# Landing times of 18 kinds of load and store in a planner that orders the five queues of a hybrid encoder layer

## The chip, the core and the metric

The kernel runs as one program on one core of a Trainium2 chip. The time is device microseconds (us) of one execution, and the figure used for the kernel before is the median of three executions. A core has five engines that work on their own instruction queues: TensorE (PE, matrix products; PEld is its loading of the stationary operand), VectorE (DVE), ScalarE (ACT), GpSimd (POOL) and SyncE (SP). Here SP issues all transfers between the main memory and the core's own memory. Each queue is worked off in the order in which it was written; an instruction that waits holds up everything behind it in its queue.

## The reference, cut to what matters

One layer, one sequence of 2048 positions, 1024 features, everything in float32. The input is normalised, projected once, and split between two groups of heads; their outputs are projected back and added to the input.

```python
h = rms_norm(x, norm_w[l])
proj = h @ w_in[l]
(dn_q, dn_k, dn_v, dn_z, dn_beta, dn_decay, sw_q, sw_k, sw_v, sw_z) = split(proj, cuts)
dn = gated_deltanet_bidir(dn_q, dn_k, dn_v, dn_beta, dn_decay, ...)   # 4 heads of 128
dn = rms_norm(dn, dn_out_norm_w[l]) * silu(dn_z)
sw = windowed_gqa_with_sinks(sw_q, sw_k, sw_v, ...) * silu(sw_z)      # 8 query heads of 64, window 128
x = x + concatenate([dn, sw]) @ w_out[l]
```

The delta-rule heads first pass q, k and v through a convolution of width 5. Then, chunk by chunk, a triangular matrix built from k, the decay and beta is inverted, and a state of 128x128 is carried along the sequence, once forward and once backward:

```python
t_inv = triangular_solve(eye + m, eye)
v_new = u_i - w_i @ state
o = (q_i * exp(g_i)) @ state + a_i @ v_new
state = state * exp(g_last) + k_dec.T @ v_new
```

## The kernel before, in words

The kernel is written as a program for the five queues, first without regard to what should come when; at the end a planner in the same file, `set_order`, lays down the order of every queue.

Phase A (`phase_a`) works in two halves of 1024 positions. Rows of x come in as tiles `xr` (for the sums of squares, and in the very first block also for transposition on PE), columns of x as tiles `xt`; both become the pairs `xhi`/`xlo`, from which every projection takes three products. Weights come in as `ws_...`. Windowed attention is interleaved with the convolution pairs (`pf_c`) and the gates (`pf_z`) as filling for PE. Results that phase B needs go to the main memory: `kq_d`, `v_d`, `zdn_d`, `zsw_d`, `mix_sw`.

Phase B (`phase_b`) handles the four delta-rule heads one after the other. For each head h:

- `pre_front(h)` runs over four groups of 512 positions. Each group loads `kq` (512 KB, two buffers), `vt` and two `dc` (decay matrices; for head 0 they were stored ready, for the others a row is loaded to all partitions), transposes k, q and v on PE (`tr` L674, `trv` L711), forms `gh` (L694), scales it on DVE into `ma` (L703), and stores half of `ma` to `m_d` (L708).
- `solve(h)` loads the diagonal blocks from `m_d` as `X` and `L` (L731, L732), solves 31 steps on DVE (L741, L745) and stores `x_d` (L746).
- `invert(h)` loads `xc` from `x_d` (L757), copies blocks on POOL and forms five products per group on PE (`pi`, L772).
- `scan(h)` walks 16 chunks in both directions. A step loads `kqc` (L810), forms `pk`, `py`, `po` on PE, and updates the state on DVE (L833). At the end `post` loads the gate `zt` (L880) and stores `mix_dn` (L882).

So a head is a chain through the main memory: `kq`, then `m_d`, `X`/`L`, `x_d`, `xc`, and then its scan. Heads alternate between two sets of `ma` buffers, so `pre_front(h+2)` follows scan(h). Between these, units of the output projection of the attention part fill PE: a unit loads `mxs`, sometimes `zcs`, and `xrs`, makes 12 products of 128x512 (`pcs`, L599 to L601) and stores `part`; its weights come in as `woss`. At the very end `out_dn` loads `mxd` and `xrd`, makes 12 products twice (`pcd`, L561 to L563) and stores the output; its weights come in as `wosd`.

The planner `set_order` collects all instructions, finds which depends on which, including those that must wait until a buffer is free, and gives each a duration (`cost`; 500 ns for an issue on SP). It then plays the program through forward and backward several times as a list scheduler: of the instructions that are ready on an engine, the one comes next whose time in the pass before demands it. The shortest plan of the last five forward passes is written into the queues as the order. What is planned is only the order: on the chip every instruction waits for its real inputs.

An instruction that depends on a transfer is ready, in the plan, when the issue has begun and the planned bus has become free, plus the 500 ns of the issue, plus a lag:

```python
LAG = {"PE": 205, "DVE": 140, "Activation": 160, "Pool": 120, "SP": 2400}
move[k] = count / piece * (8 + 0.148 * piece) / 16
lag = LAG[eng[k]] + move[k] + late[k] if k < n else 0
```

Here `count` is the number of elements and `piece` the number of them that lie side by side (at most 2048), so `move` is a time in ns from the size and the grain of the transfer, and `late` is 2000 for loads that spread one row over all partitions, else 0. The planned bus is busy for `move` with each transfer.

Of the kernel before, what the change touches and what calls it, by code (L numbers as in the profile page):

```python
# [927 lines left out]


ENGINES = ("PE", "DVE", "Activation", "Pool", "SP")  # L930
LAG = {"PE": 205, "DVE": 140, "Activation": 160, "Pool": 120, "SP": 2400}
SAME = {"PE": 0, "DVE": 115, "Activation": 130, "Pool": 120, None: 0}

# [4 lines left out]
def set_order(tc):  # L938


    insts, boundaries = [], []
    for i in tc.nc.cur_bb.bb.instructions:
        eng = str(i.engine).split(".")[1]
        if i.opcode == "TilePoolBoundary":
            boundaries.append(str(i))
        elif eng in ENGINES:
            insts.append((i, eng))
# [3 lines left out]
    def aps(l):  # L951
        return [a.bass_ap for a in l if hasattr(a, "bass_ap")]

    def size(a):
        r = 1
        for _, c in list(a.ap)[1:]:
            r *= c
        return r

    def run(a):  # L960
        inside = a.tensor.name in tiles and "DRAM" not in str(tiles[a.tensor.name].space)
        r = 1
        for step, c in reversed(list(a.ap)[1:] if inside else list(a.ap)):
            if step != r:
                break
            r *= c
        return min(r, 2048)
# [89 lines left out]
    for x in sorted((x for x in tc.tiles if x.tag in home and x.name in used), key=lambda x: used[x.name][0]):  # L1057
        name, bufs = home[x.tag]
        users.setdefault(name, []).extend(used[x.name])
        k = used[x.name][0]  # L1060
# [25 lines left out]
    for x in used:  # L1086
        k = used[x][0]
# [32 lines left out]
    move, late = [0.0] * total, [0.0] * total  # L1120
    nxt, prv = [[] for _ in range(total)], [[] for _ in range(total)]
    for k in range(total):
        if eng[k] == "SP":
            a = aps(insts[k][0].outs)[0]
            count = a.ap[0][1] * size(a)
            piece = min(run(x) for x in aps(insts[k][0].ins) + [a])
            move[k] = count / piece * (8 + 0.148 * piece) / 16
            spread = [x.ap[0][0] == 0 for x in aps(insts[k][0].ins)]
            late[k] = 2000 * any(spread)
        lag = LAG[eng[k]] + move[k] + late[k] if k < n else 0  # L1130
        if eng[k] == "PE" and not insts[k][0].is_transpose and "float32r" not in str(insts[k][0].ins[0].dtype):
            lag += 40
        if eng[k] == "Activation" and len(aps(insts[k][0].outs)) > 1:
            lag += 90
        for s in succ[k]:
            if eng[s] == eng[k] != "SP":
                nxt[k].append((s, SAME[eng[k]] * ((k, s) in wrote)))
            else:
                nxt[k].append((s, lag))
        for s in started[k] if k < n else ():  # L1140
            nxt[k].append((s, None))
        for s, d in nxt[k]:
            prv[s].append((k, d))
# [30 lines left out]
    def plan(order, forward):  # L1174
        to, back = (nxt, prv) if forward else (prv, nxt)
        left, at = [len(x) for x in back], [0.0] * total
        later, ready = {e: [] for e in ENGINES}, {e: [] for e in ENGINES}
        free, queue = dict.fromkeys(ENGINES, 0.0), {e: [] for e in ENGINES}
        begin, bus, held = [0.0] * total, 0.0, 0.0
# [24 lines left out]
        for _ in range(n):  # L1204
            t, e = min(
                (free[e] if ready[e] else max(free[e], later[e][0][0]), e) for e in ENGINES if ready[e] or later[e]
            )
# [38 lines left out]
    info = mybir.DependencyInfo(mybir.DependencyClass.NoSync, mybir.DependencyReason.DATA)  # L1246
    for e in ENGINES:
        for a, b in zip(queue[e], queue[e][1:]):
# [60 lines left out]
```

## Time and profile before

| | |
|---|---|
| median of 3 executions | 1278.94 us (1277.84 to 1281.57) |
| the profiled execution | 1274.25 us, span 1272.5 us from first to last instruction |
| mean granted TensorE clock | 0.992 |
| transfers | 205.34 MB, mean 161 GB/s over the span |
| busy DVE, ACT, POOL | 889.5, 703.2, 507.4 us |

Read the span in three parts: a start-up of some 20 us, phase A to about 660 to 770 us, and phase B after it. The timeline gives for each group of instructions its start, its time, its engine, the line of the kernel, the tile written and the tiles read; a bracket at the end gives the idle time of the engine just before, and what ended it. An "x4" behind a row means four instructions merged. PE products are pipelined: the next one starts before the time shown for the one before has run out, so the distance of starts is the better measure.

### The profile page before, as it was taken

The numbers are of one execution on the slowest core, as the hardware profiler recorded it, in microseconds if no ns is written. First come the engines' busy times: TensorE is split into PE (matmuls) and PEld (weight loads), VectorE is DVE, ScalarE is ACT, GpSimd is POOL, SyncE is SP. The second block draws the span as 40 slices with busy tenths as digits, with TensorE's granted clock in tenths as the row PEclk, the third lists the DMA queues.
The fourth block names the chain that finished last, engine by engine and source line by source line (L and its number), as shares of the span: only waits on it lengthen the run. The fifth ranks groups of instructions, "written<-read, shape, count | busy, mean of one in ns | idle before, by whom it ended". The sixth has DMA issues, their size and how long they took to land.

```text
span 1272.5 us, 22253 instructions
## 1 busy us (share of the span) xinstructions
PE 1219.4 (96%) x7066; PEld 1044.4 (82%) x7066; DVE 889.5 (70%) x2154; ACT 703.2 (55%) x2105; POOL 507.4 (40%) x893
## 2 busy tenths in 40 slices
PE   6999999999999999999999998998799899999998
PEld 6998877788889998787788787887688789798876
DVE  4422387999975589999986573788488879557333
ACT  6321254776644677776654425858557955566210
POOL 1330044666613398665221306613672651641000
PEclk9999999999999999999999998999899999999999
DMA  8442254322544434522137826967965974746675
GB/s 269 145 132 76 95 180 128 97 97 81 180 132 144 130 96 116 158 87 67 58 117 244 224 96 189 276 189 207 270 169 154 269 191 138 217 145 214 227 242 205
DMA packets 225510, 205.34 MB, mean 161 GB/s; under 512 B 48497, under 2 KB 175089, under 8 KB 225393
## 3 DMA queue, kind: packets, MB, share of 16 engines
q1 hardware_dynamic: 225392, 203.92, 52.7%
q8 instruction: 56, 0.92, 0.3%
q14 instruction: 62, 0.50, 0.1%
HBM read 138.79 MB, written 65.08 MB: 160 GB/s over the span
## 4 chain that ended last, share of the span: by engine, by line
PE 67%; DVE 12%; DMA 9%; ACT 7%; issue 3%; POOL 1%; SPq 0%; DVEq 0%; ACTq 0%; POOLq 0%
PE pf_c L191 4%; PE pf_c L192 4%; PE pf_c L193 4%; PE pf_z L191 4%; PE pf_z L192 4%; PE pf_z L193 4%; PE pi L772 4%; DVE acc L242 3%; PE pt L363 3%; PE pq_q L202 2%; PE pq_q L204 2%; PE pq_q L203 2%; PE pcd L561 2%; PE pcd L563 2%; PE pcd L562 2%
## 5 line engine op out<-in xcount | busy, mean ns | idle before, releaser
L191 PE MATMUL pf_c<-xhi,wh_c 128*128 128x512 f32 x384 | 151.0, 404 | 0.7 <-DVE acc L242 0.4
L192 PE MATMUL pf_c<-xlo,wh_c 128*128 128x512 f32 x384 | 150.6, 401 | 0.0
L193 PE MATMUL pf_c<-xhi,wl_c 128*128 128x512 f32 x384 | 149.1, 401 | 0.0
L242 DVE SCALAR_TENSOR_TENSOR acc<-pf_c,cw,acc 128x512 f32<-128x512 f32 (+1 forms) x192 | 140.3, 743 | 11.3 <-ACT acc L238 9.2
L358 POOL TENSOR_SCALAR pr<-pr,st 128x384 f32<-128x384 f32 (+1 forms) x128 | 80.1, 648 | 71.3 <-DVE st L356 60.0
L191 PE MATMUL pf_z<-xhi,wh_z 128*128 128x512 f32 x256 | 86.6, 401 | 0.5 <-DVE zo L215 0.5
L349 ACT ACTIVATE pr<-pr,st 128x384 f32<-128x384 f32 (+1 forms) x128 | 76.1, 596 | 19.6 <-DVE st L345 19.1
L192 PE MATMUL pf_z<-xlo,wh_z 128*128 128x512 f32 x256 | 86.2, 399 | 0.0
L191 PEld LDWEIGHTS pf_c<-xhi,wh_c 128*128 128x128 f32 x384 | 72.1, 188 | 15.3 <-DVE acc L242 1.7
L193 PE MATMUL pf_z<-xhi,wl_z 128*128 128x512 f32 x256 | 84.7, 397 | 0.0
L192 PEld LDWEIGHTS pf_c<-xlo,wh_c 128*128 128x128 f32 x384 | 72.3, 188 | 13.0
L193 PEld LDWEIGHTS pf_c<-xhi,wl_c 128*128 128x128 f32 x384 | 71.8, 188 | 13.0
L345 DVE CUSTOM_DVE_ANT_0 pr<-s,mask,sink 128x384 f32<-128x384 f32 (+1 forms) x128 | 72.5, 593 | 12.4 <-PE s L344 8.3
L367 ACT ACTIVATE ph<-pt 128x512 fp32r<-128x512 f32 x92 | 53.0, 596 | 40.9 <-PE pt L363 39.1
L826 ACT ACTIVATE yk<-py,ck 128x128 f32<-128x128 f32 x120 | 43.9, 366 | 49.5 <-PE py L821 48.4
L363 PE MATMUL pt<-ident,pr 128*128 128x128 f32 x368 | 67.2, 274 | 1.9 <-DVE q L327 1.1
L368 DVE TENSOR_TENSOR pl<-pt,ph 128x512 fp32r<-128x512 f32 x92 | 61.6, 681 | 5.1 <-ACT ph L367 5.0
L703 DVE SCALAR_TENSOR_TENSOR ma<-gh,bp,dc 128x256 f32<-128x256 f32 x128 | 54.9, 476 | 10.4 <-PE gh L694 8.7
L363 PEld LDWEIGHTS pt<-ident,pr 128*128 128x128 f32 x368 | 46.5, 140 | 17.7 <-DVE pl L368 3.0
L202 PE MATMUL pq_q<-wh_q,xhi 128*128 128x256 f32 x256 | 60.3, 285 | 0.6 <-ACT sgkv L261 0.3
L599 PE MATMUL pcs<-wohs,mhs 128*128 128x512 f32 x128 | 57.7, 451 | 2.9 <-ACT mhs L593 2.3
L814 DVE SCALAR_TENSOR_TENSOR r<-pk,negc,vs 128x128 f32<-128x128 f32 x120 | 41.5, 346 | 27.1 <-PE pk L812 26.6
(251 smaller groups left out, 3709.8 us busy)
## 6 DMA issues: line engine op xcount, KB each, us to landing
kqc<-kq_d SPq DMA_DIRECT2D x120, 128.0 KB, 3.0
ws_c<-wt SPq DMA_DIRECT2D x48, 256.0 KB, 3.3
xr<-x SPq DMA_DIRECT2D x16, 512.0 KB, 6.3
ws_z<-wt SPq DMA_DIRECT2D x32, 256.0 KB, 3.9
kq<-kq_d SPq DMA_DIRECT2D x16, 512.0 KB, 5.3
m_d<-ma SPq DMA_DIRECT2D x32, 256.0 KB, 5.4
mxs<-mix_sw SPq DMA_DIRECT2D x32, 256.0 KB, 3.8
xrs<-x SPq DMA_DIRECT2D x32, 256.0 KB, 3.6
```

The source lines that it names most:

```text
L191: T.matmul(ps, hi[:, k, cs], xhi[b][:, k], start=(k == 0), stop=False)
L192: T.matmul(ps, hi[:, k, cs], xlo[b][:, k], start=False, stop=False)
L193: T.matmul(ps, lo[:, k, cs], xhi[b][:, k], start=False, stop=(k == KC - 1))
L202: T.matmul(ps[:, :n], xh, hi[:, k, :n], start=(k == 0), stop=False)
L242: V.scalar_tensor_tensor(av, ps[:, lo:], cw[:, i, k : k + 1], av, ALU.mult, ALU.add)
L345: V.tensor_tensor_reduce(pr[j][:, :n], ps[:, :n], mask[:, lo * P : hi * P], 1.0, sink[:, hh : hh + 1], ALU.add, ALU.min, accum_out=nm[:, j ...
L349: A.activation(pr[j][:, :n], pr[j][:, :n], AF.Exp, bias=nm[:, j : j + 1], scale=-1.0, accum_out=den[:, j : j + 1])
L358: G.tensor_scalar(pr[j][:, :n], pr[j][:, :n], den[:, j : j + 1], 1.0, ALU.mult, ALU.mult)
L363: T.transpose(pt[:, j], pr[j][:, (kb - lo) * P : (kb - lo + 1) * P], ident)
L368: V.tensor_tensor(pl, ptf, ph.bitcast(F32), ALU.subtract)
L599: T.matmul(ps, mh[:, k], wh[:, k], start=(k == 0), stop=False)
L703: V.scalar_tensor_tensor(ma[d, c4][:, c], gh[:, k], bp[:, d, cc : cc + 1], gms[d][:, c : c + 1].to_broadcast([P, 2, P]), ALU.mult, ALU.mult,)
```

## The change: a table of landing times

The planner gets a table of landing times in ns by the leading letters of a tile's name. For a transfer whose output tile begins with one of these names followed at once by a digit, `late` becomes at least so large that the whole lag (2400 + `move` + `late`) is the table's value. The bus time `move` and the 500 ns of the issue stay as they are. Nothing else is changed: instructions, tiles, buffers and transfers are those of before, and only the order that the planner writes into the queues can differ.

```diff
 ENGINES = ("PE", "DVE", "Activation", "Pool", "SP")
+LANDS = {"m_d": 5400, "x_d": 5500, "xc": 3300, "X": 4600, "L": 4600, "lt": 4600, "kq": 5300, "vt": 5100, "dc": 6100, "zt": 5100, "mix_dn": 3900, "mxd": 4000, "xrd": 4900, "mxs": 3800, "xrs": 3600, "zcs": 3900, "kqc": 3000, "xr": 6000, "xt": 6200, "woss": 4600, "wosd": 4600}
 LAG = {"PE": 205, "DVE": 140, "Activation": 160, "Pool": 120, "SP": 2400}
...
             move[k] = count / piece * (8 + 0.148 * piece) / 16
             spread = [x.ap[0][0] == 0 for x in aps(insts[k][0].ins)]
             late[k] = 2000 * any(spread)
+            base = aps(insts[k][0].outs)[0].tensor.name
+            for form, lands in LANDS.items():
+                if base.startswith(form) and base[len(form)].isdigit():
+                    late[k] = max(late[k], 1.0 * (lands - LAG["SP"] - move[k]))
```

The table has 21 names. A tile's full name is the name in the program with an underscore and a running number behind it: the tile `mix_dn` is called `mix_dn_100`, and the weight tiles of the last projection `wosd_0_0_...`. Neither has a digit right behind the table's name, so these two entries apply to nothing; and no tile begins with `lt`. The other 18 apply to 440 of the kernel's 887 transfers.

## The prediction

> **What bounds the kernel now.** I read the busy shares first, then the chain of work that ended last, then the transfers by line, then stretches of phase B, and last the order on single queues.
>
> ```profile
> PE 1219.4 (96%) x7066; PEld 1044.4 (82%) x7066; DVE 889.5 (70%) x2154; ACT 703.2 (55%) x2105; POOL 507.4 (40%) x893
> ...
> PE 67%; DVE 12%; DMA 9%; ACT 7%; issue 3%; POOL 1%; SPq 0%; DVEq 0%; ACTq 0%; POOLq 0%
> ```
>
> PE is the bound almost everywhere: it idles 1272.5 - 1219.4 = 53 us in all. Transfers are 9% of the last chain. A new order can add no work and remove none; it can only move these 53 us, the clock that is lost beside them, and the time in which PE looks busy but waits inside a chain. The stretches show where they lie.
>
> ```profile
> 500.00:600.00 100.00, 99.32 (x495) 79.63 (x493) 97.70 (x220) 73.77 (x187) 68.61 (x94) 1.00 0.34 107
> ...
> 780.00:810.00 30.00, 24.13 (x154) 21.77 (x153) 19.51 (x48) 25.84 (x108) 22.54 (x46) 0.89 0.92 270
> ...
> 890.00:925.00 35.00, 26.97 (x145) 21.66 (x145) 17.36 (x52) 17.98 (x70) 20.04 (x45) 0.90 0.93 261
> 925.00:985.00 60.00, 58.21 (x416) 53.77 (x416) 51.79 (x153) 39.39 (x144) 30.59 (x56) 0.97 0.55 160
> 985.00:1020.00 35.00, 30.34 (x201) 25.82 (x201) 30.23 (x95) 32.18 (x144) 22.91 (x48) 1.00 0.92 259
> ...
> 1080.00:1110.00 30.00, 27.36 (x176) 22.58 (x177) 17.82 (x57) 18.80 (x76) 19.00 (x46) 1.00 0.72 210
> ```
>
> Columns: stretch, length, busy PE, PEld, DVE, ACT, POOL, then clock, share of the DMA engines, GB/s. Phase A is full (99.32 of 100). PE loses 5.9, 8.0, 4.7 and 2.6 us in four short stretches, the passages between heads: one scan has ended, `invert` of the next head and `pre_front` of the one behind it run together, and in the first three the DMA engines are at 0.92 to 0.93. The scans between are full (58.21 of 60). So the change matters in the passages, where many of its transfers land.
>
> ```profile
> xr<-x SPq DMA_DIRECT2D x16, 512.0 KB, 6.3
> ...
> kq<-kq_d SPq DMA_DIRECT2D x16, 512.0 KB, 5.3
> m_d<-ma SPq DMA_DIRECT2D x32, 256.0 KB, 5.4
> ...
> x_d<-X SPq DMA_DIRECT2D x4, 512.0 KB, 5.5
> xc<-x_d SPq DMA_DIRECT2D x32, 64.0 KB, 3.3
> ...
> X<-m_d SPq DMA_DIRECT2D x4, 256.0 KB, 4.6
> ```
>
> The last column is the median from issue to landing; the table of the change carries these medians (for `xr` 6.0). Before, by the kernel's formula, the plan's lag is 3.68 us for `xr` and `x_d` (128 pieces of 1024), 3.74 for `kq` (256 of 512), 3.26 for `m_d` (512 of 128), 4.03 for `X` (2048 of 32), 2.81 for `xc` (512 of 32). The change adds 2.32, 1.82, 1.56, 2.14, 0.57 and 0.49.
>
> **The change part by part.** *The first rows of x.* The table gives one price to a form, whatever else is under way.
>
> ```profile
> 0.74 0.39 SPq L109 DMA_DIRECT2D xr<-x  x1
> ...
> 2.12 0.91 SPq L181 DMA_DIRECT2D ws_kv<-wkv  x2
> ...
> 4.40 1.06 ACT L124 ACTIVATE xhi<-xr 128x1024 fp32r<-128x1024 f32 x1 [2.38 <-DMA xr<-x]
> 6.31 0.77 ACT L182 ACTIVATE wh_kv<-ws_kv 128x272 fp32r<-128x272 f32 x2 [0.76 <-DMA ws_kv<-wkv]
> 8.30 1.06 ACT L124 ACTIVATE xhi<-xr 128x1024 fp32r<-128x1024 f32 x1 [1.23 <-DMA xr<-x]
> ...
> 7.85 1.97 PE L131 MATMUL xt<-ident,xr 128*128 128x128 f32 x8 [7.85 <-DVE xr L127]
> ```
>
> With nothing ahead of it, `xr` lands 4.40 - 0.74 = 3.66 us after its issue, as the old formula has it. The new plan has it ready at 0.5 + 6.0 = 6.5 us, and the first `ws_kv` (fourth in the fixed order of loads, behind 2.77 us of planned bus; lag 2.4 + 0.39) at 6.05, the second at 6.44. So ACT is given the two casts `wh_kv` ahead of the square of `xr`. On the chip they cannot start before 6.31 and take 0.77, so the square starts at 7.08 instead of 4.40, and PE's first transposes 2.7 us later than 7.85. What covers it: the second `xr` lands only at 8.30, and later rows pace the block, so the slack comes back in part. Bounds 0 and +2.7; between them I take **+1.3**. The same entry moves no other exposed load: the later `xr` and `xt` are fetched beneath a full PE.
>
> The Trainium skill, "DMA: Bandwidth & Descriptors", section "Anatomy of one DMA — SWDGE (gpsimd) path", fits, for the other issue path, a constant 2.0 us plus bytes at 436 GB/s, which as an estimate is 3.2 us for 512 KB. It speaks against a price per form: 3.66 us agrees with it within 0.5, and by it the plan's excess is 3.3 us and not 2.8, and the term with the same cover +1.5.
>
> *The stalled `kq`.* The largest wait of PE after the start-up is for this form.
>
> ```profile
> 780.94 0.66 PE tr L674 x4
> ...
> 784.16 6.08 DMA kq<-kq_d
> 790.38 1.09 PE tr L674 x4
> 791.46 0.43 PE po L830 x2
> 791.89 0.43 PE py L821 x2
> 792.32 1.28 PE pi L772 x6
> 793.60 0.43 PE po L839 x2
> ...
> 790.38 1.09 PE L674 MATMUL tr<-ident,kq 128*128 128x128 f32 x4 [3.86 <-DMA kq<-kq_d]
> ```
>
> The plan had put the transposes 0.5 + 3.74 = 4.24 us behind the issue; they were ready after 6.22. PE stood 3.86 us. Behind them waited `po`, `py` and `pi`, which do not read this `kq`: 0.43 + 0.43 + 1.28 + 0.43 = 2.57 us. With 5.8 us in the plan they go ahead, so at most these 2.57 us fill the gap: **-2.6**. Bounds 0 (their own inputs are late too: `po` at 793.60 needs an output of ACT) and -3.9. The clock falls as well: 0.89 in 30 us is 3.3 us, of which the four groups already carry half of their 2.57, as they ran at half clock (four transposes took 1.09 us against 0.66 at 780.94). Of the other 2.0 us I take half, **-1.0**; bounds 0 and -2.0. The Trainium skill, "TensorE: Matmul & The Clock Gate", section "Part 1: The HAM clock gate (the "warmup" mystery)", has the clock halved after an idle window of about 3.4 us. The 3.86 us agree; if the gap falls to 1.3 us, by this rule all 2.0 come back and the sum below is 1.0 lower.
>
> *The stalled `xrs`.* PE's other wait for a transfer comes by way of DVE.
>
> ```profile
> 909.82 5.71 DMA mix_dn<-zt
> 915.60 0.33 SPq L880
> 915.98 6.72 DMA xrs<-x
> 922.78 0.69 DVE xrs L602
> ...
> 923.72 0.49 PE L812 MATMUL pk<-S,kqc 128*128 128x128 f32 x2 [2.94 <-DVE S L837]
> ```
>
> SP stands at the load of `zt` until the store `mix_dn` has freed its buffer; `xrs` goes out behind it. `mix_dn` is one of the entries that match nothing, and `xrs` goes from 3.07 to 3.6 only, far from 6.72. I take 0; bounds -2.9 and 0.
>
> *The chain of a head.* The plan's price is now too high where it was too low. It counts the 500 ns of the issue and the wait for its bus ahead of the lag, while the trace's landing runs from the start of the issue and holds the queueing: 784.16 + 6.08 = 790.24, and the transposes start at 790.38. So each of the five links `kq`, `m_d`, `X`, `x_d`, `xc` is planned at least 0.5 us behind its own median, 2.5 us a head. Whoever reads a link is queued behind other work chosen to fill that time, and the filling comes in lumps:
>
> ```profile
> 895.92 0.40 PE L599 MATMUL pcs<-wohs,mhs 128*128 128x512 f32 x1
> 896.15 0.39 PE L600 MATMUL pcs<-wohs,mls 128*128 128x512 f32 x1
> ```
>
> Products start 0.23 us apart, a unit of 12 is 2.8 us, and `invert`, once its `xc` is there, stands behind it; DVE and ACT get the unit's cast and subtraction in front as well. In a scan this costs nothing, since 58.21 of 60 us are full whatever the order. In a passage no scan covers it, and the next scan starts later by as much. Three passages follow a chain (890, 985, 1080): 3 x 2.5 = **+7.5**. Bounds: with the whole shift of 1.56 + 2.14 + 0.57 + 1.82 + 0.49 = 6.6 us per head, +19.8; on the other side, if better placed readers remove the waits for engines in these passages, half of 8.0 + 4.7 + 2.6, -7.7. I take the overcharge, since the part of the shift that only corrects the price should cost nothing.
>
> The rest of the 440 transfers (`kqc` 2.83 to 3.0; `vt`, `zt`, `mxs`, `zcs`, `woss`, `mxd`, `xrd` by 0.6 to 2.0 us) are prefetched beneath full stretches: 0, with the same bounds of both signs as above.
>
> Sum: 1.3 - 2.6 - 1.0 + 7.5 = +5.2 us on the profiled 1274.25, so 1279.4. The median of the runs is 4.7 us above that execution (1278.94), so the forecast is **1284.1 us**. A measurement can tell about 0.3%, 3.8 us, from no change.
>
> **The rivals.** *Faster: the plan stops putting readers ahead of their data.* For it speaks that the waits named are for forms in the table. Then the `kq` gap goes whole with its clock (-3.9 - 2.0), half the idle time of the three later passages too (-7.7), and the start-up costs 1.3: -12.3, or 1266.6; with the half of it that I think likely, about 1273. Against it: in the passages the DMA engines are at 0.92 or more, so the readers wait for bytes, and no order brings them sooner. It decides for this side if PE's idle time in the passages falls below some 15 us.
>
> *No change that can be told.* PE has 1219 us of work in any order; two waits of PE on a transfer make up 4.9 us only, and `mix_dn`, `wosd` and `lt` are not retimed at all, so the change does less than its table says. Then +1.3 and -3.6 are left, and some of the 7.5: 1276 to 1282, centre 1279.
>
> *Much slower.* Longer links make the chain of a head dearer in the plan's backward pass, so solve steps are pulled ahead of the scan's state updates on DVE (51.79 of 60 us busy beside the scan); scans stretch, and the whole 6.6 us per head are paid: 19.8 + 2.7 = +22.5, or 1301. This is the far end of the forecast's own case.
>
> **How the numbers follow.** Slower 0.47 (forecast and its far end, own range 1282.8 to 1299), faster 0.35, no change 0.18. The range takes the forecast's case up to 1298 and the faster one down to half-way beyond its likely size, 1266.
>
> **What would show it.** The start-up: ACT's first square of `xr` behind `wh_kv`, at about 7 us, PE's first transposes at about 10. `kq`: no wait of PE on it above 2 us. Passages: scans of heads 1 to 3 starting each some 2.5 us later against the end of the scan before. I am wrong if PE's idle time in the passages shrinks, if the first square still starts at 4.4, or if a stretch of phase A loses more than 3 us.

## The result and the profile after

| | before | after |
|---|---|---|
| median | 1279.33 us (1277.84 to 1281.57, 4 runs) | 1295.40 us (1294.31 to 1297.89, 4 runs) |
| ratio to before | | 1.0133, 95% interval 1.0116 to 1.0149 |
| the profiled execution, its span | 1274.25 us, 1272.5 us | 1296.39 us, 1294.5 us |

The change costs 16 us by the medians and 22 us between the two profiled executions. Below, the spans of executions are compared; the one of before is 5 us below its median, the one of after 1 us above.

The busy shares of after, the line that answers to the first one shown of before:

```profile
span 1294.5 us, 22212 instructions
...
PE 1225.2 (95%) x7066; PEld 1045.0 (81%) x7066; DVE 892.3 (69%) x2154; ACT 705.7 (55%) x2105; POOL 511.8 (40%) x893
```

PE idles 1294.5 - 1225.2 = 69.3 us instead of 53.1, so 16 of the 22 us are idle time; the other 6 are in a PE that is busy for longer with the same 7066 products. Who ended the idle time, before and then after (engine and line, whom it waited for, us in total, times, longest):

```profile
PE tr L674 <- DMA kq<-kq_d: 4.9, 4, 3.9
PE gh L694 <- DVE ma L703: 3.7, 3, 2.4
...
PE po L830 <- ACT yk L826: 0.6, 2, 0.3
```

```profile
PE gh L694 <- DVE ma L703: 7.8, 6, 2.0
PE po L830 <- ACT yk L826: 6.1, 8, 2.0
...
PE tr L674 <- DMA kq<-kq_d: 0.8, 1, 0.8
```

What the table was written against has gone: 4.1 of 4.9 us of waiting for `kq`. Waits for engines have taken its place, and not one of the larger ones names a transfer.

*The start.* ACT's and PE's timeline of after:

```profile
6.29 0.43 ACT L182 ACTIVATE wh_kv<-ws_kv 128x272 fp32r<-128x272 f32 x1 [4.28 <-DMA ws_kv<-wkv]
7.14 0.43 ACT L182 ACTIVATE wh_kv<-ws_kv 128x272 fp32r<-128x272 f32 x1 [0.42 <-DMA ws_kv<-wkv]
7.47 1.04 ACT L124 ACTIVATE xhi<-xr 128x1024 fp32r<-128x1024 f32 x1
...
11.00 1.97 PE L131 MATMUL xt<-ident,xr 128*128 128x128 f32 x8 [11.00 <-DVE xr L127]
```

The square of the first `xr` stands behind two casts of weights, at 7.47 instead of 4.40, and PE begins 3.2 us later (11.00 against 7.85). It is made up soon, as the start of the first gate product shows. These are the rows of the gate's third product, `pf_z` L193, before and after; behind the shortest, median and longest duration stand the first and the last start:

```profile
L193 PE MATMUL pf_z<-xhi,wl_z x256: 388/393/581, 91.5 to 774.0; 128*128 128x512 f32 x128
```

```profile
L193 PE MATMUL pf_z<-xhi,wl_z x256: 388/393/585, 91.9 to 782.3; 128*128 128x512 f32 x128
```

At the first gate product 0.4 us of the 3.2 are left, which is less than executions differ there (90.9 to 93.1 in kernels with the order of before up to this point). At the last one, which closes the work of phase A, after is 8.3 us late; from there to the end of the span it takes 1294.5 - 782.3 = 512.2 us against 1272.5 - 774.0 = 498.5. So between these two executions **8.3 us are lost in phase A and 13.7 us in phase B**. This division is used for all kernels below. Since the execution of before is 5 us below its median, each such figure can hold some us that no kernel as a whole loses; the medians further down give 7.0 and 9.1.

*Phase A.* The stretch 400 to 500, before and then after (columns as in the prediction):

```profile
400.00:500.00 100.00, 99.86 (x690) 91.67 (x689) 74.94 (x183) 64.40 (x165) 59.88 (x95) 1.00 0.36 104
```

```profile
400.00:500.00 100.00, 96.56 (x668) 87.69 (x667) 69.39 (x174) 59.72 (x156) 55.35 (x85) 1.00 0.32 94
500.00:600.00 100.00, 97.41 (x481) 77.47 (x480) 97.50 (x213) 73.91 (x186) 67.77 (x97) 1.00 0.34 109
```

PE idles 3.3 us more from 400 to 500 and 1.9 us more from 500 to 600. From 400 to 500 DVE gets 5.6 us less done, and from 500 to 600 it is busy at 97.5 of 100, as it was before (97.7), so it cannot make that up; this is argued from the busy times, and no run tests it. SP issues no transfer with a new price between 380 and 620 us.

*Phase B.* A passage is the time from the last `pk` (L812) of one scan to the first of the next. These are rows of L812 alone for the two long passages, before and then after; "(x0)" shows that no `pk` starts in the stretch, so its length is that of the passage less some tenths. Behind PE and PEld stand the clock, the share of the DMA engines and GB/s:

```profile
890.30:923.60 33.30, 0.00 (x0) 0.00 (x0) 0.90 0.93 264
1002.10:1024.80 22.70, 0.00 (x0) 0.16 (x1) 1.00 0.85 236
```

```profile
903.90:943.10 39.20, 0.00 (x0) 0.00 (x0) 0.83 0.85 235
1020.50:1052.20 31.70, 0.00 (x0) 0.09 (x1) 0.95 0.87 258
```

They are 5.9 and 9.0 us longer, with the share of the DMA engines at 0.85 and 0.87 instead of 0.93 and 0.85. That is not all of phase B: the first `pk` of head 0 starts 33.8 us behind the last `pf_z` instead of 21.1, and the scans then take part of that back. What goes with the longer first passage is seen on SP's queue. Before, the store of the solved blocks and the first load that reads it, and then SP's wait between them:

```profile
897.26 0.64 SPq L746 DMA_DIRECT2D x_d<-X  x1
...
903.89 0.92 SPq L757 DMA_DIRECT2D xc<-x_d  x2
```

```profile
SPq L757 <- DMA x_d<-X: 2.2, 1, 2.2
```

Before, the load stood at the head of the queue 2.2 us ahead of its data. After:

```profile
912.36 0.61 SPq L746 DMA_DIRECT2D x_d<-X  x1
...
922.95 0.53 SPq L654 DMA_DIRECT2D kq<-kq_d  x1
923.57 0.56 SPq L757 DMA_DIRECT2D xc<-x_d  x1
```

```profile
SPq L603 <- DVE xrs L602: 4.0, 1, 4.0
SPq L654 <- PE tro L878: 3.7, 1, 3.7
```

Now 11.2 us lie between store and load instead of 6.6. The plan takes the store for 6.0 us and has put a store of `part` and a load of `kq` ahead of `xc`. They wait 4.0 us for DVE and 3.7 us for PE, and `xc` waits with them: 4.6 us more than before between store and load, beside 5.9 us more in the passage. PE in turn stands at the head of its own queue for ACT:

```profile
920.39 1.50 PE L878 MATMUL tro<-ident,oacc 128*128 128x128 f32 x5 [3.22 <-ACT oacc L875]
```

### The profile page after: what moved, and what is told of

Read it like the earlier page. It is cut to its first block, busy times and chain, and to the rows that moved or that the text cites. A ratio compares the mean times of both kernels' runs of the same rounds, so it can differ in the third digit from the quotient of the medians.

```text
span 1294.5 us, 22212 instructions
## 1 busy us (share of the span) xinstructions
PE 1225.2 (95%) x7066; PEld 1045.0 (81%) x7066; DVE 892.3 (69%) x2154; ACT 705.7 (55%) x2105; POOL 511.8 (40%) x893
## 4 chain that ended last, share of the span: by engine, by line
PE 39%; DVE 7%; ACT 4%; POOL 4%; DMA 3%; issue 2%; SPq 1%; DVEq 0%; POOLq 0%; ACTq 0%
PE pi L772 4%; PE pcd L561 2%; PE pf_z L192 2%; PE pcd L562 2%; PE pcd L563 2%; PE pf_z L191 2%; PE pf_z L193 2%; PE py L821 2%; PE po L830 2%; PE po L839 2%; PE pf_c L191 2%; PE pf_c L192 2%; PE pcs L599 2%; PE pf_c L193 2%; PE pk L812 2%
## 5 line engine op out<-in xcount | busy, mean ns | idle before, releaser
L242 DVE SCALAR_TENSOR_TENSOR acc<-pf_c,cw,acc 128x512 f32<-128x512 f32 (+1 forms) x192 | 140.2, 743 | 15.6 <-ACT acc L238 13.3
L193 PE MATMUL pf_c<-xhi,wl_c 128*128 128x512 f32 x384 | 150.6, 402 | 0.0
L193 PE MATMUL pf_z<-xhi,wl_z 128*128 128x512 f32 x256 | 85.3, 398 | 0.0
L191 PEld LDWEIGHTS pf_c<-xhi,wh_c 128*128 128x128 f32 x384 | 72.1, 188 | 15.6 <-DVE acc L242 2.6
L193 PEld LDWEIGHTS pf_c<-xhi,wl_c 128*128 128x128 f32 x384 | 72.2, 188 | 12.6
L684 POOL TENSOR_TENSOR nk<-ssk,pw 128x4 f32<-128x4 f32 x16 | 16.4, 1028 | 145.6 <-DVE ssk L683 145.5
L703 DVE SCALAR_TENSOR_TENSOR ma<-gh,bp,dc 128x256 f32<-128x256 f32 x128 | 55.3, 476 | 14.2 <-PE gh L694 10.9
```

What stands on the lines that cost most here:

```text
L191: T.matmul(ps, hi[:, k, cs], xhi[b][:, k], start=(k == 0), stop=False)
L193: T.matmul(ps, lo[:, k, cs], xhi[b][:, k], start=False, stop=(k == KC - 1))
L242: V.scalar_tensor_tensor(av, ps[:, lo:], cw[:, i, k : k + 1], av, ALU.mult, ALU.add)
L703: V.scalar_tensor_tensor(ma[d, c4][:, c], gh[:, k], bp[:, d, cc : cc + 1], gms[d][:, c : c + 1].to_broadcast([P, 2, P]), ALU.mult, ALU.mult,)
```

## The experiments

Two theories: **prices**, in which the new price of an entry makes the loss at the place where its readers stand; and **a draw**, in which any change of any price gives a new order for the whole program, some orders are worse, and the entries do not matter.

### Which half of the program: the two plans joined

The planner runs with and without the table, and each queue takes one order up to the planned start of head 0's first transposes and the other from there on (`planned` is the planning code of after as a function of its table):

```diff
-    end, begin, queue = best
+    (end, begin, queue), (_, _, then) = planned({}), planned(LANDS)
+    cut = min(begin[k] for x in used if x.startswith("tr0_") for k in used[x])
+    for e in ENGINES:
+        queue[e] = [k for k in queue[e] if begin[k] < cut] + [k for k in then[e] if begin[k] >= cut]
```

> The planner runs twice, without the table and with it. Every queue takes the order planned without the table up to the planned start of the first transposes of head 0 (tr, L674), and the order planned with the table for the rest. Against the profile of before, the profile of after loses 8.3 us of progress of PE between 430 and 620 us (phase A) and 13.7 us net from the passages between heads on. Theory one, the two losses are separate and add up: phase A as before, phase B late by 13.7 us, so about 1.1% above before. Theory two, phase B is paced by its own chains and the loss of phase A only uses up slack there, so the passages alone make the whole: about 1.3% above. Theory three, the loss of phase B is only a consequence of the queue positions that phase A left behind: within 0.3% of before.

Measured: 1.0071 (1.0048 to 1.0095), 9.1 us. That is more than theory three allows and less than theory one's 1.1%, which was taken from the two profiled executions. The counterpart has `planned(LANDS), planned({})`:

> The counterpart: the order planned with the table up to the start of head 0's first transposes, the order planned without it for the rest. Theory one, losses that add up: 8.3 us, 0.65% above before. Theory two, phase B is paced by itself: within 0.3% of before. Theory three, phase A makes all of it: about 1.3% above.

Measured: 1.0055 (1.0033 to 1.0076), 7.0 us, as theory one has it. The sum of both excesses is 1.26%, the whole change 1.33%: the losses are separate and add up. In the traces the first kernel takes 1284.8 - 772.1 = 512.7 us from the last `pf_z` to the end, as after does; the second reaches it at 780.1, as after about does, and then takes 497.8, as before does.

### Which entries: the table in parts

```diff
-LANDS = {"m_d": 5400, "x_d": 5500, ...}
+LANDS = {"xr": 6000, "xt": 6200}
```

> The table keeps only xr and xt, the two entries that act in phase A. Theory one, a wrong price costs where its readers stand: the first square of ACT late as in after, the loss of 8.3 us of phase A there, phase B as before, 0.4 to 0.7% above before. Rival, any change of the prices is a new draw of the whole order: losses or gains of up to 1% of either sign, in phase B too, where no price has changed.

Measured: 1.0025 (1.0010 to 1.0040), less than the 0.4 to 0.7% of theory one. The table without these two:

```diff
-LANDS = {..., "xr": 6000, "xt": 6200, ...}
+LANDS = {...}
```

> The table without xr and xt: all entries of phase B. Theory one: the start and phase A as before, phase B late by 10 to 15 us, 0.8 to 1.2% above before. Rival, a new draw of the whole order: phase A loses or gains some us too, though no price of phase A has changed, and the sum is anywhere within 1.5%.

Measured: 1.0171 (1.0132 to 1.0210), above both theories and above the whole table. The rest of the table divided: the links of a head's chain alone, and everything but the links.

```diff
-LANDS = {"m_d": 5400, "x_d": 5500, ...}
+LANDS = {"m_d": 5400, "x_d": 5500, "xc": 3300, "X": 4600, "L": 4600, "kq": 5300}
```

> The table keeps only the links of a head's chain: kq, m_d, X, L, x_d, xc. Theory one, the overcharge of the links makes the passages longer: the passages lose 8 to 14 us as in after, about 0.6 to 1.1% above before apart from phase A. Rival, a new draw: the loss of the passages is not tied to these entries, so the two halves of the table (this one and the one without the chain) lose without regard to which half holds the links.

Measured: 1.0167 (1.0138 to 1.0195), 21 us, of which 12 lie in phase A by the division below.

```diff
+LANDS = {"lt": 4600, "vt": 5100, "dc": 6100, "zt": 5100, "mix_dn": 3900, "mxd": 4000, "xrd": 4900, "mxs": 3800, "xrs": 3600, "zcs": 3900, "kqc": 3000, "xr": 6000, "xt": 6200, "woss": 4600, "wosd": 4600}
```

> The table without the links of the chain: vt, dc, zt, mxd, mxs, xrd, xrs, zcs, kqc, woss, xr, xt. Theory one: the passages as before within 3 us; the start late by 2 to 3 us and made up by 42 us. Rival, a new draw: passages lose 5 us or more although no link has another price.

Measured: 1.0039 (1.0014 to 1.0063).

### No entry at all: 10 ns on the lag of every transfer

```diff
+LANDS = {}
-LAG = {"PE": 205, "DVE": 140, "Activation": 160, "Pool": 120, "SP": 2400}
+LAG = {"PE": 205, "DVE": 140, "Activation": 160, "Pool": 120, "SP": 2410}
```

> No table; SP's lag in the planner is 2410 ns instead of 2400, a shift of 10 ns that no reader on the chip can feel. It changes 4536 lines of PE's order against 5412 with the table. Theory one, the prices of the table make the loss: within 0.4% of before. Rival, any change of the prices is a new draw of the order, and before is a lucky one: 0.5 to 1.5% above before, with losses in phase A's second half or in the passages, like those of after.

Measured: 1.0024 (1.0010 to 1.0039), which is within the 0.4% that the theory of prices allows. With 2390 in the same place:

> The same with 2390 ns, 4335 lines of PE's order changed. Theory one: within 0.4% of before. Rival, a new draw: another loss of 0.5 to 1.5%, in other places than with 2410. If one of the two is 0.3% or more below before, before is no lucky draw but one of many.

Measured: 1.0058 (1.0039 to 1.0077), which is not. So a change of 10 ns, far below every wait named here, costs up to 0.6%: there is a draw. The row of `pf_z` L193 shows where it acts. In this order, one fence each: rows of x only, no rows of x, chain only, no chain, 2410, 2390.

```profile
L193 PE MATMUL pf_z<-xhi,wl_z x256: 388/393/582, 91.0 to 776.4; 128*128 128x512 f32 x128
```

```profile
L193 PE MATMUL pf_z<-xhi,wl_z x256: 388/393/586, 92.7 to 789.6; 128*128 128x512 f32 x128
```

```profile
L193 PE MATMUL pf_z<-xhi,wl_z x256: 387/393/586, 90.6 to 786.4; 128*128 128x512 f32 x128
```

```profile
L193 PE MATMUL pf_z<-xhi,wl_z x256: 387/393/587, 91.7 to 779.9; 128*128 128x512 f32 x128
```

```profile
L193 PE MATMUL pf_z<-xhi,wl_z x256: 387/393/587, 93.4 to 786.8; 128*128 128x512 f32 x128
```

```profile
L193 PE MATMUL pf_z<-xhi,wl_z x256: 388/393/581, 91.5 to 782.2; 128*128 128x512 f32 x128
```

With the spans, this divides each kernel as the result was divided (phase A is the last start less 774.0; phase B is span less last start, less 498.5):

| table | links priced | phase A | span | phase B |
|---|---|---|---|---|
| whole (after) | yes | +8.3 | 1294.5 | +13.7 |
| no rows of x | yes | +15.6 | 1304.8 | +16.7 |
| chain only | yes | +12.4 | 1295.5 | +10.6 |
| rows of x only | no | +2.4 | 1280.2 | +5.3 |
| no chain | no | +5.9 | 1277.0 | -1.4 |
| none, lag 2410 | no | +12.8 | 1279.2 | -6.1 |
| none, lag 2390 | no | +8.2 | 1281.8 | +1.1 |

Each figure is one execution, and that of "no rows of x" is the slowest of its four, 6.5 us above their median. In the five kernels that carry the order of before up to the cut (the joined one above and the four below; the first transposes of head 0 start at 672 to 678 us there) the last start lies between 772.1 and 778.1, so some 4 us of either column are scatter or come from the order behind the cut. **Phase A is a draw.** It loses 8 to 13 us by a shift of 10 ns, and least, within the scatter, with the only two entries whose loads act there. **Phase B goes by prices, with a wide spread**: the three tables with the links lose 10.6 to 16.7 us, the four without them -6.1 to +5.3. The joined kernels fit this, with +14.2 us (512.7 - 498.5) where phase B was planned with the table and -0.7 where it was not. The spread of 11 us among the four without links is a draw as well, so a single order says little of a few us.

### How much of the price: the chain alone in four sizes

In all four the order of before stands up to the cut, so that the draw of phase A is out, and only the six links have another price in the plan for the rest:

```diff
-                    late[k] = max(late[k], 1.0 * (lands - LAG["SP"] - move[k]))
+                        late[k] = 1.0 * (lands - LAG["SP"] - move[k])
```

> Order of before up to the start of head 0's first transposes, so that phase A is out of the comparison; for the rest the order planned with the prices of the chain's links alone (kq, m_d, X, L, x_d, xc) at the table's values. So far phase B lost 10.7 to 16.4 us in the four kernels with these prices and -6.1 to +5.4 us in the four without. Theory one, the plan's longer links become later readers: phase B loses 11 to 14 us, 0.8 to 1.1% above before. Rival, a draw: -6 to +5 us.

Measured: 1.0065 (1.0039 to 1.0091), 8.3 us; less than the 11 to 14 expected, the interval reaches 11.6. With `lands - 500` in the same line:

> As the run with the chain's links alone, with 500 ns taken off each of the six prices: what the planner counts twice, since the landing of the trace runs from the start of the issue. Overcharge, as in the prediction: the loss of phase B goes, at most 3 us of it are left. Theory one by size, every ns that the plan adds to a link counts, right or too much: 4.1 of 6.6 us a head are left, so 60% of the loss of the run with the full prices, 6 to 9 us. Rival, a draw: no relation to that run.

Measured: 1.0061 (1.0038 to 1.0085), 7.8 us, at the least 4.9. The overcharge theory, which left at most 3 us, falls. From the run before, this one cannot be told apart. With the factor 2.0:

> As the run with the chain's links alone, with twice the rise of the table over the old lag on each link (13.2 us a head instead of 6.6). Theory one: phase B loses twice as much, 22 to 28 us, 1.7 to 2.2% above before. Overcharge: more than twice, since all of the second rise is overcharge. Rival, a draw: -6 to +16 us, without regard to the size.

Measured: 1.0193 (1.0167 to 1.0220), 24.7 us. It is in theory one's range, but three times the 8.3 us of factor 1, and "more than twice" was the sign of overcharge; since the intervals (21.4 to 28.1 and 5.0 to 11.6) still hold a ratio of two, this run does not decide. With the factor -0.5:

> The other sign: each link of the chain is priced below the old lag by half of the table's rise (3.3 us a head less). Theory one, the price becomes the time: phase B gains, 3 to 7 us, 0.2 to 0.5% below before, with more waits of PE on kq. The author's premise, that readers ahead of their data cost: phase B loses 3 us or more, the wait on kq above the 4.9 us of before. Rival, a draw: -6 to +5 us.

Measured: 0.9977 (0.9963 to 0.9991), 2.9 us **faster than before**, and so faster than both kernels. The gain is smaller than what 10 ns on the lag cost. The rows of L812 for the two long passages, in the order of the price: factor -0.5, less 500 ns, factor 1, factor 2. Before stands between the first two, with 33.3 and 22.7.

```profile
892.40:917.10 24.70, 0.00 (x0) 0.00 (x0) 1.00 0.97 279
1002.50:1028.10 25.60, 0.00 (x0) 0.15 (x1) 1.00 0.83 233
```

```profile
897.30:933.80 36.50, 0.00 (x0) 0.03 (x1) 0.91 0.95 274
1010.00:1036.90 26.90, 0.00 (x0) 0.10 (x1) 1.00 0.84 238
```

```profile
894.20:934.20 40.00, 0.00 (x0) 0.00 (x0) 0.87 0.94 255
1009.20:1039.70 30.50, 0.00 (x0) 0.11 (x1) 1.00 0.84 248
```

```profile
898.10:949.50 51.40, 0.00 (x0) 0.08 (x1) 0.83 0.81 223
1016.40:1053.50 37.10, 0.00 (x0) 0.00 (x0) 0.95 0.78 231
```

Both passages together: 50.3, (before) 56.0, 63.4, 70.5, 88.5 us. With the price of the links per head at -3.3, 0, 4.1, 6.6 and 13.2 us, their sum grows with every step, though the transfers are the same; the second alone does not (25.6, 22.7, 26.9, 30.5, 37.1). Phase B as a whole, divided as above, is longer than before by +1.7, (before) 0, +5.4, +8.8 and +21.2 us. So the profiled execution with factor -0.5 does not show the gain, which rests on the medians of 12 and 17 executions.

The passages are not the loss itself. In the table without the links they are

```profile
897.90:934.00 36.10, 0.00 (x0) 0.00 (x0) 0.95 0.97 275
1006.10:1036.60 30.50, 0.00 (x0) 0.17 (x1) 1.00 0.90 254
```

together 66.6 us, 10.6 more than before, which was the sign of a draw in that run, and yet its phase B is 1.4 us shorter. What goes with the links' prices in every kernel is the time from the store `x_d` to the first `xc`, summed over the four heads by SP's timeline: 26.4 to 32.8 us in the six kernels with the links at the table's prices or twice the rise, 19.2 to 23.2 us in the other eight, before (21.4) and the run with less 500 ns (20.6) among them. That the run with less 500 ns loses 7.8 us all the same is not explained by this link.

How a price becomes time is barest in head 0, where the queue has little else to do. SP's timeline with factor -0.5, then with factor 2:

```profile
767.54 0.32 SPq L746 DMA_DIRECT2D x_d<-X  x1
770.12 2.02 SPq L757 DMA_DIRECT2D xc<-x_d  x4
```

```profile
775.11 0.32 SPq L746 DMA_DIRECT2D x_d<-X  x1
...
777.81 1.21 SPq L810 DMA_DIRECT2D kqc<-kq_d  x2
...
781.49 2.54 SPq L810 DMA_DIRECT2D kqc<-kq_d  x4
784.07 2.43 SPq L757 DMA_DIRECT2D xc<-x_d  x3
```

With factor -0.5 the store has landed 2.6 us after its issue at the latest, since the load that reads it goes out then. In a plan that takes it for 7.8 us (3.68 + 2 x 1.82 + 0.5), that same load comes 9.0 us after it, behind loads of `kqc` for the next scan. Between these ends the price is not the only cause: the distance is 2.6 us with less 500 ns, 4.4 in before and 5.9 with factor 1.

The author's premise, that readers ahead of their data are what costs, is not borne out: with prices 3.3 us a head too low PE waits for `kq` 4.4 us in all, with the right ones 0.2, and the first is 11 us faster by the medians (1276.55 against 1287.60). More such waits than in before (4.9 us) did not come with the lower prices, though they were expected, so the premise is tested by this one comparison only.

## Why the prediction was right, and where its size was off

Forecast 1284 us, range 1266 to 1298; measured 1295.4, on the forecast side and inside the range, with a loss three times as large: 16 us for 5.2. By the joined kernels phase A lost 7.0 us, for which the forecast had +1.3, and phase B 9.1, for which it had 7.5 - 2.6 - 1.0 = +3.9. So each phase makes half of the miss.

- *The start, +1.3.* The order was as derived (square behind the two casts, at 7.47 where 7.08 was worked out; transposes 3.2 us late for 2.7). The cover was better than assumed: 0.4 us are left at the first gate product. The table with the rows of x alone as a whole costs 0.25%.
- *The `kq` wait, -2.6, and the clock, -1.0.* The wait went (4.9 to 0.8 us). The gain did not come: the same passage now has five other waits, of 2.0, 1.8, 1.3, 1.0 and 0.9 us, and a clock of 0.85 in 780 to 815 against 0.90 before in the same stretch, though none of its waits is above 2.0 us. A wait removed at the head of one queue was replaced by waits in others.
- *The stalled `xrs`, 0.* Nothing here can be told apart from the rest of the passage; left open.
- *The chain of a head, +7.5.* The mechanism was in the main the one described: readers of a link queued behind other work while no scan covers it. That it acts in phase B is shown by the tables with and without the links; that the passages carry all of it is not shown, as the table without links has long passages too. The size came out near: 8.3 us (5.0 to 11.6) with the links alone, `kq` among them. Its reason did not, and so the nearness is luck: the term was built on the overcharge, because "the part of the shift that only corrects the price should cost nothing". Taking the 500 ns off each link left 7.8 of 8.3 us, where this reason left nothing. So more than the overcharge counts, but the 19.8 us of the whole shift were not paid either. The third passage did not grow (14.8 and 13.5 us).
- *The rest of the table, 0, and phase A untouched.* "The same entry moves no other exposed load" was true of the loads and beside the point: phase A lost 8.3 us in the traces and 7.0 by the medians, by a new order in a part whose prices had not changed. This term, put at nothing, is the largest miss of the sum. The prediction named this as what would make it wrong (a stretch of phase A losing more than 3 us), but had no term for it. In the runs with 10 ns phase A loses 8 to 13 us, so a shift of that size is enough for it.
- *The rivals.* "Faster" rested on readers placed ahead of their data; their wait on `kq` went, and PE's idle time still grew from 53.1 to 69.3 us. "Much slower" (1301) came nearer to the time than the forecast did, but by another way: it put the loss into stretched scans, and the scans became shorter (head 0's 94.8 to 87.3 us, from the starts of the first and last `pk`), and it had no loss in phase A beyond the start.

What stays open: why most other orders lose in phase A, and by which link the run with less 500 ns loses. In the seven orders of the table above it was never earlier than before, so the order of before is a favourable one there; which of its choices makes it so was not tried.

## What to carry to other kernels

A planner for in-order queues does not become better by truer prices alone: a price that is too low can make one reader wait for its data, while a price that is too high, or true only where many transfers are under way, can put other work ahead of it, whose own waits come on top. On the chain that sets the pace of this kernel, prices below the old ones did better than the traced medians (1276.55 against 1287.60 us). Any change of a plan should be held against a tiny shift in the same plan: 10 ns alone cost this kernel 0.2 to 0.6%.

## What the runs showed of the hardware

The landing of one form is no constant: the 512 KB store `x_d`, with a median of 5.5 us in the profile of before, was readable after 2.6 us in head 0 of the run with lower prices, with the DMA engines at 0.49 in that time, and after 6.6 us in the second head of before, in a passage where they were at 0.93.

PE's clock also halves without a long gap. In after, PE's timeline has

```profile
907.90 1.22 PE L694 MATMUL gh<-kq 128*128 128x256 f32 x4 [1.95 <-DVE ma L703]
...
912.29 0.63 PE L601 MATMUL pcs<-wols,mhs 128*128 128x512 f32 x1
912.72 0.63 PE L599 MATMUL pcs<-wohs,mhs 128*128 128x512 f32 x1
```

and these are the stretches of one us in which the clock changes (behind POOL's busy time stand the clock, the share of the DMA engines and GB/s):

```profile
908.00:909.00 1.00, 1.00 (x5) 0.80 (x6) 0.54 (x3) 0.65 (x3) 1.00 (x2) 0.91 0.95 283
915.00:916.00 1.00, 1.00 (x5) 0.78 (x4) 0.00 (x0) 0.00 (x0) 0.00 (x0) 0.68 1.15 339
922.00:923.00 1.00, 1.00 (x6) 0.76 (x5) 0.43 (x2) 1.00 (x5) 0.36 (x1) 0.73 0.75 226
```

A mean of 0.91 over the first is a full clock until 908.82 and half of it from there on: 0.9 us after the end of a wait of 1.95 us, with no other wait above 0.2 us in the 5 us before. From then on, products start 0.43 us apart instead of 0.23. The Trainium skill, "TensorE: Matmul & The Clock Gate", "Part 1: The HAM clock gate (the "warmup" mystery)", speaks of an idle window of about 3.4 us. Here one wait of 1.95 us was enough. In the same way the clock is full again from 915.64 and halved from 922.46, each 6.82 us behind the change before it; all twelve changes found in this way in after lie multiples of 3.41 us apart. The wait of 3.22 us that ended at 920.39 thus met a full clock at its end and a halved one 2.1 us later, so the length of a wait alone does not tell what it costs. The clock of the first long passage is 1.00 with factor -0.5 and 0.83 with factor 2.
